# A transformer layer on one core: second-half feature blocks in three rounds, one copy on ScalarE, one low part on VectorE, two key scalings behind a weight split

## The chip, the cores and the metric

The kernel runs on one core of a Trainium2 chip. A core has five engines with a queue of instructions each: TensorE (PE: matrix products and transposes into PSUM), VectorE (DVE), ScalarE (ACT), GpSimd (POOL) and SyncE (SP, which here issues most of the transfers). The engines wait for one another by semaphores. The metric is the time of one execution on the device in microseconds, as a median over runs.

## The reference

One layer over 1024 latent tokens of width 1024 with 256 context tokens ahead of them. Cut to what matters here:

```python
h_lat = rms_norm(x, norm1_g) * (1 + sc1) + sh1        # sh1, sc1 from silu(c) @ w_mod + b_mod
h_ctx = rms_norm(ctx, norm1_g) * (1 + csc1) + csh1    # the same from c_ctx
rq, rk, rv, rg, dq, dk, dv = split(h @ w_in)          # seven blocks of 512 columns
# retention: rotary on rq, rk; per direction and head, over chunks of 128 tokens
S = S * c_dec + (kc * k_dec).T @ vc
o = (qc @ kc.T * intra) @ vc + (qc * q_dec) @ S
# differential attention: softmax(q1 k1) - lam * softmax(q2 k2), times dv
x = x + g1 * (concat(silu(rg) * norm(o), norm(att)) @ w_out)
x = x + g2 * conv_ffn(rms_norm(x, norm2_g) * (1 + sc2) + sh2)
out = rms_norm(x, final_g)
```

Everything is float32. The change lies in `h_lat` and `h_ctx` (the opening), and where the retention keys `rk`, the gates `rg` and the states `S` are computed.

## The kernel before, in words

**Products.** A float32 product is made of three passes (`passes`, lines 133 to 135): each operand is split into a high part of a shorter type (a copy or cast on ACT) and a low part, the difference (a subtraction on DVE), and PE adds high by high, high by low and low by high. So an operand is ready when its low part is.

**The opening.** The 1024 token rows are eight tiles of 128; tiles 0 to 3 are the first half (`xs0`), tiles 4 to 7 the second half (`xs1`). Each row tile gets its sum of squares on ACT (`square`, L561), a short DVE step and a power on POOL (`power`, lines 115 and 116: their result is the factor of the norm), and is scaled on DVE (`scale`, L567). Then `modulate` turns it over, one feature block d of 128 features at a time, for four tiles together: four transposes on PE into a PSUM buffer (`pt`, L573), the modulated high part on ACT (`hT`, L576), a modulated plain copy on DVE (`tmp`, L578), and the low part from copy and high part (L580) on DVE for d = 0, 1 and even d, on POOL for the other odd d. There are three transpose buffers `pt` and two copy buffers `tmp`, so a transpose can wait for the copy of three blocks earlier, and a copy for the low part of two blocks earlier. The second half's blocks are called B0 to B7 below, and the last one of the first half A7.

While the blocks are made, PE multiplies what is there: for k = 0 to 7 the products of feature block k for token tiles 0 and 1 and then for 2 and 3 (`part_products`, lines 617, 619 and 623, six products each time) with the block of w_in that holds the values of the differential attention. In the last two rounds, k = 6 and 7, the second half's blocks stand in pairs in front of these products: B0, B1 | B2, B3 | B4, B5 | B6, B7. Then come token tiles 4 and 5, three passes for each k (24 products each), with a function `between` that puts other work between them: in tile 4 the stores of token tiles 2 and 3 and the context's squares, powers and scalings, in tile 5 the context's eight feature blocks (`cT`, made by `modulate` too, two tiles together).

`in_order(begin)` holds PE, DVE, ACT and SP to the order in which the opening is written, up to the end of token tile 5. POOL is free of it. Outside of the opening a scheduler sets the order, and `order_only(a, b)` is a constraint for it: a comes after b, without a wait.

**Weights.** Each later block of w_in is streamed in four slices (`split_slice`): a load, the high part `whi` on ACT (L194), the low part `wlo` on DVE (L195).

**Retention keys and gates.** With the rotary tables in place, `transposed` makes the retention keys, for four heads in two token halves: 24 products into `pl`, then `rotated` (two ACT copies of half the partitions into `xb`, L443; the DVE steps `xa`, L449 and the following), and one tile later `natural_copy` turns the rotated tile over (`pk`, L461), copies it on ACT (L463) and stores it. Then the gates' block is streamed, and for its natural tiles (products `pn`) the function `states` runs beside: for each step of the recurrence it loads a tile `kvs` of keys and values that was stored before, scales the keys by their decay on ACT (`scaled_keys`, `ks`, L326), and multiplies (`pu`, L342).

Of the kernel before, what the change touches and what calls it, by code (L numbers as in the profile page):

```python
# [11 lines left out]
AF = mybir.ActivationFunctionType  # L12
ALU = mybir.AluOpType
# [4 lines left out]
P = 128  # L18
D = 1024
KD = D // P  # L20
# [54 lines left out]
def kernel(  # L75
# [81 lines left out]
    with ExitStack() as p1:  # L157
# [24 lines left out]
        mcol = hp.tile([P, KD, 2, 2], F32, name="mcol")  # L182
        csil = hp.tile([P, KD, 2], F32, name="csil")

        low_parts, newest_raw = [], []

        def split_slice(src, pool, spare=False):
            raw = ev.tile([P, 2, 512], F32, name="raw", tag="xhl") if spare else wr.tile([P, 2, 512], F32, name="raw")
            newest_raw[:] = newest_raw[-1:] + [nc.sync.dma_start(out=raw, in_=src)]
            if spare:  # L190
                order_only(newest_raw[1].ins, newest_raw[0].ins)
            whi = pool.tile([P, 2, 512], F32R, name="whi")
            wlo = pool.tile([P, 2, 512], F32R, name="wlo")
            nc.scalar.copy(whi, raw)  # L194
            low_parts.append(nc.vector.tensor_tensor(out=wlo, in0=raw, in1=r32(whi), op=ALU.subtract))  # L195
            return whi, wlo

# [49 lines left out]
        class Pair:  # L247
# [46 lines left out]
            def turn(self, behind=None):  # L294
# [9 lines left out]
                o = self.g % 2 * 2 * P  # L304
                nc.sync.dma_start(out=yr_d[self.g // 2][:, :, self.h, o : o + 2 * P].rearrange("p a (s l) -> p a s l", s=2), in_=r32(yr))

        states_at, last_y, turned_q, newest, first_turned, newest_read, rotations, made = {}, [], {}, [], [], [], [], {}

        def states(heads):


            one = [(0, 0, (0, 1)), (1, 0, (1, 0))]
            for g in range(1, 5):
                one += [(0, g, (0, 1) if g < 4 else (0,)), (1, 5 - g, (1, 0) if g < 4 else (1,))]
            seq = [(h, *step) for h in heads for step in one]
            kvs = []

            def load_until(n):
                for i in range(len(kvs), min(n, len(seq))):
                    h, d, g, _ = seq[i]  # L320
                    kvs.append(kvs[-1] if g == 0 and d == 1 else load_kv(h, g, "kvs", 0))

            def scaled_keys(i):
                h, d = seq[i][:2]
                ks = rt.tile([P, 2, P], F32, name="ks")
                nc.scalar.activation(ks, kvs[i][:, 0], AF.Copy, scale=kd[:, h, d : d + 1])  # L326
                return ks

            load_until(4)
            yield  # L330
            ahead = scaled_keys(0)
            for i, (h, d, g, cs) in enumerate(seq):
                if i % len(one) == 0:
                    states_at[h] = [rt.tile([P, NT, P], F32, name=f"S{e}") for e in range(2)]
                    last, made = [None, None], [-2, -2]
                load_until(i + 4)
                kv, ks = kvs[i], ahead
                if i + 1 < len(seq):
                    ahead = scaled_keys(i + 1)
                pu = tr_tile([P, 2, P], "pu")  # L340
                for c in cs:
                    mm(pu[:, c, :], ks[:, c, :], kv[:, 1, c, :], start=True, stop=True)  # L342
# [115 lines left out]
        def natural_copy(xa, h, hf):  # L458
            pk = pst.tile([P, 4, P], F32, name="pk", tag="tr")
            for i in range(4):  # L460
                nc.tensor.transpose(pk[:, i, :], xa[:, i * P : (i + 1) * P], ident)  # L461
            st = ev.tile([P, 4, P], F32, name="st")
            nc.scalar.copy(st, pk)  # L463
# [66 lines left out]
        with ExitStack() as p0:  # L530
# [35 lines left out]
            def scale(xt, col, c0=0, c1=D):  # L566
                nc.vector.tensor_scalar(out=xt[:, c0:c1], in0=xt[:, c0:c1], scalar1=sm[:, col : col + 1], scalar2=None, op0=ALU.mult)  # L567

            def modulate(tiles, d, who, hi, lo):
                n = len(tiles) * P  # L570
                pt = pst.tile([P, 512], F32, name="pt", tag="tr")
                for i, t in enumerate(tiles):
                    nc.tensor.transpose(pt[:, i * P : (i + 1) * P], t[:, d * P : (d + 1) * P], ident)  # L573
                sh = mcol[:, d, 0, who : who + 1]
                a = mcol[:, d, 1, who : who + 1]
                nc.scalar.activation(hi, pt[:, :n], AF.Identity, scale=a, bias=sh)  # L576
                tmp = xp.tile([P, 512], F32, name="tmp", bufs=2)
                nc.vector.tensor_scalar(out=tmp[:, :n], in0=pt[:, :n], scalar1=a, scalar2=sh, op0=ALU.mult, op1=ALU.add)  # L578
                eng = nc.gpsimd if d % 2 and d > 1 else nc.vector
                eng.tensor_tensor(out=lo, in0=tmp[:, :n], in1=r32(hi), op=ALU.subtract)  # L580

            mods, wts, rws = mm_tile("pr").rearrange("p (a b) -> p a b", a=2), {}, {}
# [96 lines left out]
            for k in range(KD):  # L679
# [21 lines left out]
                    scale(xs1[2], 8)  # L701
                    scale(xs1[3], 9)
                if k >= 6:
                    latents(1, 4 * (k - 6))
                    latents(1, 4 * (k - 6) + 1)
                if 0 < k < 5:
                    load_row(k + 3)
                n = k + 4
# [22 lines left out]
                    power(6)  # L731
                    power(7)
                if k == 4:
                    scale(xs1[1], 7)
                    square(xs1[3], 9)
                    power(9)
                if k == 5:
                    first.close()
                    cp = pctx.enter_context(tc.tile_pool(name="cp", bufs=1, side="right"))
# [2 lines left out]
                        xc.append(xp.tile([P, D], F32, name="xc", tag="wt", bufs=5))  # L742
                        nc.sync.dma_start(out=xc[t], in_=ctxt[t * P : (t + 1) * P, :])
                if k >= 6:
                    latents(1, 4 * (k - 6) + 2)
                    latents(1, 4 * (k - 6) + 3)
            rtab = load_rope(1)
            for t in range(2):
                store(t, part[t])

            def between(t, k):
                if (t, k) == (4, 1):
                    for i in (2, 3):
                        store(i, part[i])
                if t == 4 and k in (3, 5):
# [1009 lines left out]
```

## Time and profile before

| | us |
|---|---|
| median of three runs | 1378.36 (1378.05, 1378.36, 1380.14) |
| the profiled execution's own time | 1378.18 |
| its span, first to last instruction | 1376.4 |
| mean granted clock of PE | 0.998 |
| PE busy | 1358.7 (99%) |
| DVE, ACT, POOL busy | 1000.9, 730.7, 339.8 |

The page and the views of the trace tell times of one execution in microseconds from the span's start, and 1.8 us lie around the span. A row of busy times gives an engine, its time, its share of the span and its instructions. In a table by stage each row begins with the stretch A:B and its length; then follow, each with its instruction count, busy PE, PE's weight loads (PEld), DVE, ACT and POOL, then the granted clock, the busy share of the DMA engines and the GB/s. A wait is written "waiting instruction <- instruction that ended it: total, count, mean". In a table of rows in order of time each row has its start, its duration, engine, line, operation, output <- inputs with their shapes, and how many instructions follow one another there; a bracket at the end is the idle time ahead of it, and what ended it. For several instructions the duration runs from the first's start to the last's end. Groups give busy time and mean ns of one, then the engine's idle time ahead of them.

### The profile page before, as it was taken

The page shows a single profiled execution, that of the slowest core. Times are in us where ns is not written, and L with a number is a line of the kernel's source. Part 1 is how long each engine was busy: PE and PEld are TensorE (multiplying, and loading weights), DVE is VectorE, ACT ScalarE, POOL GpSimd, SP SyncE. Part 2 cuts the span into 40 slices and gives each one's busy share as a digit, 9 for nine tenths or more (in the row PEclk, how much of TensorE's full clock was granted, in tenths as well). Part 3 has the DMA queues.
Part 4 walks back from the last instruction along what each step waited for, and adds up shares of the span by engine and source line. Part 5 has one row for each costly group of instructions (what it writes and reads, how often), then busy time and mean ns, then how long its engine had stood idle before and what let it go on. Part 6 is the DMA issues. An engine that isn't in the chain of part 4 may idle for free.

```text
span 1376.4 us, 19496 instructions
## 1 busy us (share of the span) xinstructions
PE 1358.7 (99%) x7026; PEld 1143.8 (83%) x7026; DVE 1000.9 (73%) x1473; ACT 730.7 (53%) x1396; POOL 339.8 (25%) x375
## 2 busy tenths in 40 slices
PE   9999999999999999999999999999999999999997
PEld 6788888888988899998888778888888888888886
DVE  4655874425776998895458997878777887799857
ACT  4652312434665889985146554455544555454534
POOL 1310005403665424410201633322333220000001
PEclk9999999999999999999999999999999999999999
DMA  9546897654556767624410233233232325963523
GB/s 377 202 166 209 292 323 247 183 169 143 169 168 200 169 172 177 145 37 153 146 46 31 87 113 107 108 115 111 96 115 100 115 78 171 375 225 114 177 92 123
DMA packets 97192, 218.32 MB, mean 159 GB/s; under 512 B 9732, under 2 KB 31236, under 8 KB 96584
## 3 DMA queue, kind: packets, MB, share of 16 engines
q1 hardware_dynamic: 86216, 185.98, 39.6%
q0 software_dynamic: 10304, 29.65, 9.0%
q10 hardware_dynamic: 576, 1.44, 0.3%
q8 instruction: 55, 0.90, 0.3%
q14 instruction: 41, 0.34, 0.1%
HBM read 160.40 MB, written 56.64 MB: 158 GB/s over the span
## 4 chain that ended last, share of the span: by engine, by line
PE 90%; DVE 4%; DMA 2%; ACT 2%; issue 1%; SPq 0%; POOL 0%; POOLq 0%; ACTq 0%; DVEq 0%
PE chain L133 5%; PE chain L134 5%; PE chain L135 5%; PE pv L939 5%; PE pA L907 5%; PE c L134 5%; PE c L135 5%; PE c L133 5%; PE pl L135 4%; PE pl L133 4%; PE pl L134 4%; PE pn L135 3%; PE pn L134 3%; PE pn L133 3%; PE third L133 3%; PE third L135 3%
## 5 line engine op out<-in xcount | busy, mean ns | idle before, releaser
L133 PE MATMUL pl<-hT,whi 128*128 128x512 f32 x256 | 105.4, 412 | 0.0
L133 PE MATMUL chain<-T,whi 128*128 128x512 f32 x264 | 103.2, 391 | 2.2 <-ACT ua L1395 1.5
L134 PE MATMUL chain<-T,whi 128*128 128x512 f32 x264 | 102.9, 390 | 0.0
L135 PE MATMUL chain<-T,wlo 128*128 128x512 f32 x264 | 102.6, 389 | 0.0
L910 DVE TENSOR_REDUCE mt<-pA 128x1 f32<-128x1280 f32 x64 | 95.2, 1489 | 7.1 <-PE pA L907 6.8
L135 PE MATMUL pl<-hT,wlo 128*128 128x512 f32 x256 | 100.2, 391 | 0.0
L134 PE MATMUL pl<-hT,whi 128*128 128x512 f32 x256 | 100.0, 391 | 0.0
L135 PE MATMUL c<-whi,ghl 128*128 128x512 f32 x232 | 90.3, 389 | 0.0
L133 PE MATMUL c<-whi,ghl 128*128 128x512 f32 x232 | 90.3, 389 | 0.0
L134 PE MATMUL c<-wlo,ghl 128*128 128x512 f32 x232 | 90.3, 389 | 0.0
L907 PE MATMUL pA<-ks,qhl 128*128 128x512 f32 (+1 forms) x384 | 89.5, 368 | 0.6 <-ACT p L914 0.5
L914 ACT ACTIVATE p<-pA,mt 128x1280 f32<-128x1280 f32 x64 | 85.4, 1335 | 8.6 <-DVE mt L910 8.5
L1127 ACT CAST whi<-cmb 128x512 fp32r<-128x512 f32 x62 | 38.4, 622 | 82.0 <-PE chain L134 65.0
L1300 POOL TENSOR_TENSOR cmb<-wrb 128x512 f32<-128x512 f32 x19 | 26.6, 1400 | 223.6 <-DMA wrb<-w_up 134.5
L907 PEld LDWEIGHTS pA<-ks,qhl 128*128 128x128 f32 x384 | 67.9, 189 | 12.7 <-ACT p L914 1.3
L939 PE MATMUL pv<-va,aT 128*128 128x128 f32 x640 | 77.0, 276 | 0.2 <-ACT aT L933 0.2
L1130 DVE TENSOR_TENSOR wlo<-cmb,whi 128x512 fp32r<-128x512 f32 x62 | 60.2, 972 | 20.5 <-ACT whi L1127 20.5
L939 PEld LDWEIGHTS pv<-va,aT 128*128 128x128 f32 x640 | 74.0, 192 | 0.9 <-ACT aT L933 0.8
L1127 ACT CAST whi<-wra 128x512 fp32r<-128x512 f32 x54 | 33.1, 622 | 69.6 <-PE third L134 42.4
L133 PE MATMUL third<-yT,whi 128*128 128x512 f32 x168 | 65.6, 391 | 1.8 <-DVE ub L1404 1.8
L135 PE MATMUL third<-yT,wlo 128*128 128x512 f32 x168 | 65.5, 390 | 0.0
L134 PE MATMUL third<-yT,whi 128*128 128x512 f32 x168 | 65.5, 390 | 0.0
(331 smaller groups left out, 3878.2 us busy)
## 6 DMA issues: line engine op xcount, KB each, us to landing
wm<-w_mod SPq DMA_DIRECT2D x32, 512.0 KB, 5.2
raw<-w_in SPq DMA_DIRECT2D x27, 512.0 KB, 6.0
wra<-w_up SPq DMA_DIRECT2D x24, 512.0 KB, 3.3
wrb<-w_up SPq DMA_DIRECT2D x22, 512.0 KB, 3.5
W<-w_down SPq DMA_DIRECT2D x44, 256.0 KB, 6.5
ad<-s SPq DMA_DIRECT2D x20, 512.0 KB, 3.3
wra<-ad SPq DMA_DIRECT2D x20, 512.0 KB, 3.8
kvs<-kvg SPq DMA_DIRECT2D x36, 256.0 KB, 3.2
```

The costliest lines, as they stand in the source:

```text
L133: mm(ps, lh, rh, start=first, stop=False, skip_group_check=more)
L134: mm(ps, lh, rl, start=False, stop=False, skip_group_check=more)
L135: return mm(ps, ll, rh, start=False, stop=last, skip_group_check=more)
L907: mm(self.pa[m][:, c0:c1], self.q[:, m, i, qs], self.k[:, m, c0:c1], start=(i == 0), stop=(i == 1))
L910: nc.vector.tensor_reduce(out=self.mt[:, m : m + 1], in_=self.pa[m][:, :LK], axis=AX.X, op=ALU.min)
L914: nc.scalar.activation(self.p[m], self.pa[m][:, :LK], AF.Exp, scale=-1.0, bias=self.mt[:, m : m + 1], accum_out=self.s[:, m : m + 1])
L939: mm(self.pv, self.aT[:, c, :], self.v[:, c, :], start=(c == 0), stop=(c == NKT - 1))
L1127: cast = nc.scalar.copy(hi, src)
L1130: lows.append(nc.vector.tensor_tensor(out=lo, in0=src, in1=r32(hi), op=ALU.subtract))
L1300: nc.gpsimd.tensor_tensor(out=s1, in0=b1, in1=b2, op=ALU.add)
```

## The change

What it does:

1. Order of the scalings (k = 4): the square and the power of x tile 7 are written ahead of the scaling of tile 5, not behind it.
2. Rounds: the second half's blocks stand as B0 | B1, B2 | B3, B4 | B5 in the rounds k = 6 and 7, and B6 and B7 follow within token tile 4, after its second and its third k.
3. B4's plain copy is made on ACT, by the function that makes the high part, and not on DVE.
4. B7's low part is made on DVE, not on POOL.
5. The stores of token tiles 2 and 3 stand behind token tile 4's third k, not its second.
6. Three order constraints: the sixth key copy after the gates' first high part, the last but one rotation's first DVE step after the gates' first low part, and the first two key scalings after the second half copy of the last rotation. The first two name pairs that stood in this order before.

```diff
-            def modulate(tiles, d, who, hi, lo):
+            def modulate(tiles, d, who, hi, lo, late=False):
...
-                nc.vector.tensor_scalar(out=tmp[:, :n], in0=pt[:, :n], scalar1=a, scalar2=sh, op0=ALU.mult, op1=ALU.add)
-                eng = nc.gpsimd if d % 2 and d > 1 else nc.vector
+                if late and d == 4:
+                    nc.scalar.activation(tmp[:, :n], pt[:, :n], AF.Identity, scale=a, bias=sh)
+                else:
+                    nc.vector.tensor_scalar(out=tmp[:, :n], in0=pt[:, :n], scalar1=a, scalar2=sh, op0=ALU.mult, op1=ALU.add)
+                eng = nc.gpsimd if d % 2 and d > 1 and (d, late) != (KD - 1, True) else nc.vector
...
-                modulate((xs0, xs1)[half][t0:t1], d, 0, hT[0][half][:, d, t0 * P : t1 * P], hT[1][half][:, d, t0 * P : t1 * P])
+                modulate((xs0, xs1)[half][t0:t1], d, 0, hT[0][half][:, d, t0 * P : t1 * P], hT[1][half][:, d, t0 * P : t1 * P], half == 1)
...
                 if k >= 6:
-                    latents(1, 4 * (k - 6))
-                    latents(1, 4 * (k - 6) + 1)
+                    for d in ((0,), (3, 4))[k - 6]:
+                        latents(1, d)
...
                 if k == 4:
-                    scale(xs1[1], 7)
                     square(xs1[3], 9)
                     power(9)
+                    scale(xs1[1], 7)
...
                 if k >= 6:
-                    latents(1, 4 * (k - 6) + 2)
-                    latents(1, 4 * (k - 6) + 3)
+                    for d in ((1, 2), (5,))[k - 6]:
+                        latents(1, d)
...
             def between(t, k):
-                if (t, k) == (4, 1):
+                if t == 4 and 0 < k < 3:
+                    latents(1, k + 5)
+                if (t, k) == (4, 2):
                     for i in (2, 3):
                         store(i, part[i])
...
         last_rk = transposed(wg, rk_d, rtab, 64, RET_SCALE, 0, by_head, True)
+        slice0 = len(low_parts)
         wg = stream_block(3)
+        order_only(key_copies[5].ins, high_parts[slice0].ins)
+        order_only(rotations[-2][1].ins, low_parts[slice0].ins)
+        rk_turned = rotations[-1][0][1]
...
         order_only(copied_at[0], stops[first_stop].ins)
+        for made_key in keyed[:2]:
+            order_only(made_key.ins, rk_turned.ins)
```

What is left out of the diff collects the instructions that these constraints name (`high_parts`, `key_copies`, `keyed`).

PE in the opening, round k = 6, before: `pt_646` is B0 and `pt_655` B1; `pn_204` and `pn_205` are the products of token tiles 0 and 1, `hT00_177` the first half's high parts.

```order
L573 MATMUL pt_646<-ident_69,xs1_0_206 128x128
L573 MATMUL pt_646<-ident_69,xs1_1_207 128x128
L573 MATMUL pt_646<-ident_69,xs1_2_208 128x128
L573 MATMUL pt_646<-ident_69,xs1_3_209 128x128
L573 MATMUL pt_655<-ident_69,xs1_0_206 128x128
L573 MATMUL pt_655<-ident_69,xs1_1_207 128x128
L573 MATMUL pt_655<-ident_69,xs1_2_208 128x128
L573 MATMUL pt_655<-ident_69,xs1_3_209 128x128
L617 MATMUL pn_204<-whi_593,hT00_177 128x512
L617 MATMUL pn_205<-whi_593,hT00_177 128x512
```

The same place now, where `pt_661` is B1:

```order
L574 MATMUL pt_646<-ident_69,xs1_0_206 128x128
L574 MATMUL pt_646<-ident_69,xs1_1_207 128x128
L574 MATMUL pt_646<-ident_69,xs1_2_208 128x128
L574 MATMUL pt_646<-ident_69,xs1_3_209 128x128
L621 MATMUL pn_204<-whi_593,hT00_177 128x512
L621 MATMUL pn_205<-whi_593,hT00_177 128x512
L623 MATMUL pn_204<-wlo_594,hT00_177 128x512
L623 MATMUL pn_205<-wlo_594,hT00_177 128x512
L627 MATMUL pn_204<-whi_593,hT10_179 128x512
L627 MATMUL pn_205<-whi_593,hT10_179 128x512
L574 MATMUL pt_661<-ident_69,xs1_0_206 128x128
L574 MATMUL pt_661<-ident_69,xs1_1_207 128x128
```

B1 has moved behind the six products of token tiles 0 and 1, and so all later blocks by one place, the last two into token tile 4.

ACT from the second half's first high part to the first store of token tile 4, before: `hT_178` are the second half's high parts, `st` the copies of the stores, `sq,sm` the context's squares.

```order
L576 ACTIVATE hT_178<-pt,mcol 128x512 x8
L418 ACTIVATE st<-pn 128x512 x4
L561 ACTIVATE sq,sm<-xc 128x1024 x2
L418 ACTIVATE st<-pn 128x512
```

And now:

```order
L577 ACTIVATE hT_178<-pt,mcol 128x512 x5
L580 ACTIVATE tmp<-pt,mcol 128x512
L577 ACTIVATE hT_178<-pt,mcol 128x512
L419 ACTIVATE st<-pn 128x512 x2
L577 ACTIVATE hT_178<-pt,mcol 128x512 x2
L419 ACTIVATE st<-pn 128x512 x2
L562 ACTIVATE sq,sm<-xc 128x1024 x2
L419 ACTIVATE st<-pn 128x512
```

B4's copy is new behind its high part, and B6's and B7's high parts stand behind the first two stores.

ACT at the retention keys, before: `xb` are the half copies of the first rotations, `ks` the two key scalings, `st_2173` the copy of the first key tile.

```order
L443 ACTIVATE xb_2139<-pl_2113 64x512 x2
L326 ACTIVATE ks_2502<-kvs_2487,kd_882 128x256
L326 ACTIVATE ks_2506<-kvs_2487,kd_882 128x256
L463 COPY st_2173<-pk_2168 128x512
L443 ACTIVATE xb_2181<-pl_2146 64x512 x2
```

The rows with the scalings now, at the end of the keys, where `xb_2433` belongs to the last rotation, and `whi_2460` and `whi_2878` are high parts of streamed weights:

```order
L444 ACTIVATE xb_2433<-pl_2398 64x512 x2
L194 CAST whi_2460<-raw_2458 128x1024
L327 ACTIVATE ks_2502<-kvs_2487,kd_882 128x256
L327 ACTIVATE ks_2506<-kvs_2487,kd_882 128x256
L194 CAST whi_2878<-raw_2876 128x1024
L464 COPY st_2483<-pk_2478 128x512
```

The scalings have passed all copies and rotations of the keys and one weight split. Four short steps on the decay tables (128 by 128 and 128 by 1) on ACT have also passed two splits of the next block's weights, though no line of the diff names them.

More of the change, by code (lines that the diff above doesn't have):

```diff
@@ L183 @@
         csil = hp.tile([P, KD, 2], F32, name="csil")
-        low_parts, newest_raw = [], []
+        high_parts, low_parts, newest_raw = [], [], []
         def split_slice(src, pool, spare=False):
@@ L193, in split_slice @@
             wlo = pool.tile([P, 2, 512], F32R, name="wlo")
-            nc.scalar.copy(whi, raw)
+            high_parts.append(nc.scalar.copy(whi, raw))
             low_parts.append(nc.vector.tensor_tensor(out=wlo, in0=raw, in1=r32(whi), op=ALU.subtract))
@@ L305, in turn @@
                 nc.sync.dma_start(out=yr_d[self.g // 2][:, :, self.h, o : o + 2 * P].rearrange("p a (s l) -> p a s l", s=2), in_=r32(yr))
+        keyed, key_copies = [], []
         states_at, last_y, turned_q, newest, first_turned, newest_read, rotations, made = {}, [], {}, [], [], [], [], {}
@@ L325, in scaled_keys @@
                 ks = rt.tile([P, 2, P], F32, name="ks")
-                nc.scalar.activation(ks, kvs[i][:, 0], AF.Copy, scale=kd[:, h, d : d + 1])
+                keyed.append(nc.scalar.activation(ks, kvs[i][:, 0], AF.Copy, scale=kd[:, h, d : d + 1]))
                 return ks
@@ L462, in natural_copy @@
             st = ev.tile([P, 4, P], F32, name="st")
-            nc.scalar.copy(st, pk)
+            key_copies.append(nc.scalar.copy(st, pk))
             for i in range(2):
```

## The prediction

> **What bounds the kernel now.** I read the page's first part, then busy time by stage, then what TensorE (PE) waited for, and last the rows of time of the two places that the change touches.
>
> ```profile
> PE 1358.7 (99%) x7026; PEld 1143.8 (83%) x7026; DVE 1000.9 (73%) x1473; ACT 730.7 (53%) x1396; POOL 339.8 (25%) x375
> ...
> 45.98:64.20 18.22, 16.51 (x86) 12.55 (x86) 15.76 (x22) 10.66 (x17) 6.13 (x5) 1.00 0.57 212
> 219.00:268.00 49.00, 48.31 (x230) 39.45 (x229) 21.05 (x28) 18.71 (x30) 29.54 (x44) 1.00 0.58 178
> 64.20:219.00 154.80, 154.80 (x737) 130.06 (x736) 104.92 (x169) 51.73 (x98) 11.87 (x16) 1.00 0.73 251
> ```
>
> PE sets the time: 1358.7 of the 1376.4 us span. Of its 17.7 us of idle time the change can reach two pieces. One is the second half's feature blocks, 45.98 to 64.20 us, where PE lacks 18.22 - 16.51 = 1.71 us, the clock is granted in full, and VectorE (DVE) is nearly full, 15.76 of 18.22. The other is the retention keys and the first gate tiles, 219 to 268 us, 0.69 us. Between them PE never rests (154.80 of 154.80), so what the opening gains can arrive there whole.
>
> What PE waited for in the two:
>
> ```profile
> PE pt L573 <- DVE xs L567: 0.9, 1, 0.9
> PE pt L573 <- DVE tmp L578: 0.8, 1, 0.8
> PE pn L134 <- DVE wlo L195: 0.4, 1, 0.4
> PE pk L461 <- DVE xa L449: 0.3, 1, 0.3
> ```
>
> Two waits hold the opening, both for DVE: the scaling of x tile 7, and a scaled copy that still occupies a transpose buffer. I call the second half's feature blocks B0 to B7, and the first half's last one A7. PE's rows:
>
> ```profile
> 47.84 0.66 PE L573 MATMUL pt<-ident,xs 128*128 128x128 f32 x3
> 49.36 0.97 PE L573 MATMUL pt<-ident,xs 128*128 128x128 f32 x5 [0.86 <-DVE xs L567]
> ...
> 55.77 0.66 PE L573 MATMUL pt<-ident,xs 128*128 128x128 f32 x4 [0.79 <-DVE tmp L578]
> 56.19 0.70 PE L617 MATMUL pn<-whi,hT 128*128 128x512 f32 x2
> ...
> 57.65 1.04 PE L573 MATMUL pt<-ident,xs 128*128 128x128 f32 x8
> ...
> 63.87 0.50 PE L135 MATMUL pn<-whi,hT 128*128 128x512 f32 x1
> 64.20 0.40 PE L133 MATMUL pn<-whi,hT 128*128 128x512 f32 x1
> ```
>
> B0's first three transposes start at 47.84, the fourth at 49.36. B5 starts at 55.77, when B2's copy is done. The start at 64.20 belongs to the next token tile: it is the mark by which I measure the gain. A block's four transposes cost 0.42 us (55.77 to 56.19), six products 1.46 (56.19 to 57.65).
>
> **The change, part by part.**
>
> *Order of the scalings.* DVE and GpSimd (POOL) before B0:
>
> ```profile
> 46.08 0.20 ACT L561 ACTIVATION_READ_ACCUMULATOR sq<-xs 128x1 f32 x1
> 46.64 0.74 DVE L567 TENSOR_SCALAR xs<-xs,sm 128x1024 f32<-128x1024 f32 x1
> 47.30 0.14 DVE L115 TENSOR_SCALAR sm<-sm 128x1 f32<-128x1 f32 x1
> 47.53 0.99 POOL L116 TENSOR_TENSOR sm<-sm,mhalf 128x1 f32<-128x1 f32 x1 [4.29 <-DVE sm L115]
> 48.55 0.75 DVE L567 TENSOR_SCALAR xs<-xs,sm 128x1024 f32<-128x1024 f32 x1 [0.44 <-POOL sm L116]
> ```
>
> Tile 7's sum of squares is ready at 46.28 (46.08 + 0.20), but its small DVE step stands behind tile 5's scaling and runs at 47.30; the power follows on POOL until 48.52, and tile 7's scaling at 48.55. The change puts the small step first: 46.64 to 46.78, power to about 47.9, and DVE, doing tiles 5 and 6 meanwhile at 0.67 to 0.74 each, is free at about 48.1. Tile 7 is scaled by 48.85 instead of 49.30, and B0's fourth transpose starts at 48.9 instead of 49.36: **0.45 us**.
>
> *Rounds.* B0 stands alone now, then B1 and B2, B3 and B4, B5, and B6 and B7 within the first token tile's products. The same 32 transposes and the same products run; two more change-overs between them cost up to 0.1 us each. What counts is when DVE has freed each buffer (there are three):
>
> ```profile
> 50.84 1.53 DVE L578 TENSOR_SCALAR tmp<-pt,mcol 128x512 f32<-128x512 f32 x2
> 52.40 1.15 DVE L580 TENSOR_TENSOR hT<-tmp,hT 128x512 fp32r<-128x512 f32 x1
> 53.47 0.80 DVE L578 TENSOR_SCALAR tmp<-pt,mcol 128x512 f32<-128x512 f32 x1
> 54.92 0.80 DVE L578 TENSOR_SCALAR tmp<-pt,mcol 128x512 f32<-128x512 f32 x1
> ```
>
> That is DVE's chain of A7's and B0's copies, B0's low part, B1's copy and, after B1's low part, B2's copy, which freed B5 at 55.72. In the new order DVE starts it 0.45 to 0.55 earlier (A7's copy at 50.3, done 51.05), so B0's copy ends at 51.8, its low part at 52.95, B1's copy at 53.75, B2's at 55.2, B3's at 56.65. PE, by the prices above and 0.08 for each change-over: six products 49.0 to 50.5; B1 to 51.0; B2 must await A7's copy, 51.1 to 51.6; products to 53.05; B3 to 53.55; B4 must await B1's copy (53.75), 53.8 to 54.3; products to 55.75; B5, which awaits B2's copy of 55.2, without a wait to 56.25; two steps of the first token tile to 57.7; B6; one step; B7 done at 59.5; five more steps of three products (about 0.23 each) to 62.95. Against 64.20 that is **1.25 us**, tile 7's 0.45 included. PE's idle time there would fall from 1.71 to about 0.8: 0.4 before the fourth transpose, 0.1 and 0.25 before B2 and B4.
>
> *B4's copy on ScalarE (ACT), B7's low part on DVE.*
>
> ```profile
> L578 DVE TENSOR_SCALAR tmp<-pt,mcol 128x512 f32<-128x512 f32 x9 | 7.0, 802 | 0.1
> L576 ACT ACTIVATE hT<-pt,mcol 128x512 fp32r<-128x512 f32 x9 | 6.6, 777 | 5.9 <-PE pt L573 5.9
> L580 POOL TENSOR_TENSOR hT<-tmp,hT 128x512 fp32r<-128x512 f32 x4 | 5.1, 1286 | 10.2 <-DVE tmp L578 10.2
> L580 DVE TENSOR_TENSOR hT<-tmp,hT 128x512 fp32r<-128x512 f32 x5 | 4.8, 970 | 0.2
> ```
>
> ACT's form into the plain tile is not in this trace; its nearest row is the same function from the same buffer at 777 ns, DVE's own copy is 802. I take 0.78, with 0.62 to 1.0 as bounds. It leaves DVE 0.8 shorter and runs when B2's low part has freed the second copy buffer, 55.9 to 56.7, while PE reaches B6, which needs it, at 57.7. Queued behind it on ACT are B5's high part, the stores of token tiles 0 and 1, then B6's and B7's high parts; these end at about 60.3 and are needed at 62.2. B7's low part costs 0.69 to 1.15 on DVE in place of 1.29 on POOL and ends at about 62.4, needed at 62.7; before, it was the 0.1 us before 63.87. The skill's page "ScalarE: Activation LUTs", section "Rules for kernel authors", says that multiply and add belong on VectorE, which it calls up to about 3 times as fast in bf16. At three times 0.80 B4's copy would end near 58.3, B6 would wait 0.6, and the gain would be 0.65 (an estimate from that page); the 777 beside 802 ns speaks against it. The page "SBUF — State Buffer", section "Who interferes with whom", says that a DVE operation with two SBUF inputs and a GpSimd one that reads SBUF exclude each other for a whole instruction. The 1.15 us row began inside a POOL low part, so there is a clash, though less than a whole instruction's worth: 1286 ns is the longest that could be added and 0.46 was. By the rule each clash costs up to 0.14 more, B4 waits so much longer and the gain is 1.1.
>
> *Context behind it.* The squares of the two context tiles follow those stores on ACT, and PE transposes the context in the second token tile:
>
> ```profile
> 62.33 1.24 ACT L418 ACTIVATE st<-pn 128x512 f32<-128x512 f32 x2 [1.62 <-DMA dvd<-st]
> ...
> 67.13 0.76 DVE L567 TENSOR_SCALAR xc<-xc,sm 128x1024 f32<-128x1024 f32 x1 [0.45 <-POOL sm L116]
> ...
> 67.98 0.51 PE L573 MATMUL pt<-ident,xc 128*128 128x128 f32 x3
> ```
>
> This was just in time: scaled at 67.89, used at 67.98. Now PE comes at about 66.0 (1.25 for the gain, three products earlier in the new order). The first stores leave some 2 us earlier, so the third copy no longer waits for their DMA; I get the second context tile scaled at 65.9. This costs nothing or 0.2.
>
> *Weight slices of the next block.* The new order lets four short table steps of 0.3 us pass the last two slices on ACT:
>
> ```profile
> 93.76 1.04 ACT L194 CAST whi<-raw 128x1024 fp32r<-128x1024 f32 x1
> 93.59 2.47 DVE L195 TENSOR_TENSOR wlo<-raw,whi 128x1024 fp32r<-128x1024 f32 x2 [1.45 <-ACT whi L194]
> 97.87 0.39 PE L135 MATMUL pl<-hT,wlo 128*128 128x512 f32 x1
> ```
>
> The last low part is ready at 96.06 and needed at 97.87: 1.8 us of cover for about 0.9. All of it hangs on the context and shifts with PE. Nothing.
>
> *Key scalings and gates' slice.*
>
> ```profile
> 225.00 0.91 ACT L326 ACTIVATE ks<-kvs,kd 128x256 f32<-128x256 f32 x2 [4.48 <-DMA kvs<-kvg]
> ...
> 263.57 1.05 ACT L194 CAST whi<-raw 128x1024 fp32r<-128x1024 f32 x1 [1.12 <-DMA raw<-w_in]
> 265.93 0.50 PE L134 MATMUL pn<-wlo,hT 128*128 128x512 f32 x1 [0.43 <-DVE wlo L195]
> ...
> 267.64 1.06 PE L342 MATMUL pu<-kvs,ks 128*128 128x128 f32 x8
> ```
>
> Two scalings block ACT until 225.00 for their DMA; behind them the copies and rotations of the first key tiles are a microsecond late, for which PE has other products. Moved behind the split of 263.57 they run at 264.6 to 265.6, two us ahead of their use at 267.64. The 0.43 us wait hangs on the last slice's load, which the change does not touch; the first slice stands where it stood. I cost this at **0**; bounds are -0.7 (both waits gone) and +0.5 (the scalings, 0.91 us, in front of the last split's partner).
>
> **Sum.** 1.25 with 0.05 off for the context: 1.2 us. The profiled execution took 1378.18 (span 1376.4 and 1.8 around it), so 1377.0; the median of the runs shown is 0.18 above it, which gives **1377.2**.
>
> **Rivals.**
> - *Everything goes* (0.06): both waits of the opening with their refills (counted from start to start, 47.84 + 0.33 to 49.36 is 1.19, and 55.77 less 54.75 is 1.02; with the 0.1 and the change-overs about 2.4) and the second place's 0.7 vanish: 1378.36 - 3.1 = 1375.3. Against it: DVE must still do 15 us of work in that window.
> - *The stall only moves* (0.18): DVE is the limit; with clashes of 0.46 on three low parts its chain runs 0.8 late, B4, B6 and the context wait, and 0 to 0.6 remains: 1378.0.
> - *Slower* (0.10): ACT's queue. B4's copy waits there for DVE's B2 low part, and the stores stand ahead of B6 and B7. If DVE's chain is 1.3 us late or more, B5 to B7's high parts, stores, squares and context scaling are all late, and PE, at the context 1.9 us sooner, waits longer than it gained. If scaling stays at 67.89, the wait is 1.9 against 1.25: 1379.0. It decides from a context scaling after about 67.3.
> - *The change does nothing it says* (0.03): the order shows that it moves, so only the second place, where the slice's order is the same, is of this kind: 1378.4.
>
> **How the numbers follow.** The forecast (0.6 to 1.9 us gained, 1376.5 to 1377.8) has 0.63. The range 1375.3 to 1379.3 reaches from the first rival to the slower one, with 0.3 on top for the median's place (0.31 above the lowest of its runs). A difference of 0.2%, 2.8 us, is about what a measurement of this kernel tells from none, and nearly all of the cases lie inside: faster by more needs everything to go, 0.05; slower by more 0.04; within it 0.91.
>
> **What would show it.** Right: in PE's rows the fourth transpose of B0 about 0.45 earlier, waits there of 0.3 to 0.5, short waits before B2 and B4, the next token tile at 62.8 to 63.3, no wait of more than 0.2 at the context, and the 0.4 for the gates' last slice still there. Wrong: a wait for ACT's copy before B6, a context wait above 0.5, or a PE wait between 64 and 219 us, where none was.

## The result, and the profile after

| | runs | median, us | lowest to highest | mean |
|---|---|---|---|---|
| before | 22 | 1380.10 | 1377.94 to 1383.35 | 1380.34 |
| changed | 22 | 1377.35 | 1376.44 to 1379.67 | 1377.57 |

The ratio is 0.9980, with a 95% interval of 0.9973 to 0.9987: 1.8 to 3.7 us faster. The profiled execution of the changed kernel took 1376.93 us (span 1375.2), 1.25 less than the one of before. So the two profiled executions differ by what was forecast, and the medians by more than twice as much; the runs of before are also spread wider, over 5.4 us against 3.2. The three runs that the prediction started from (median 1378.36) were a low sample of these 22. When the two kernels ran again, on one chip, their medians lay 1.85 us apart (ratio 0.9987, further down). One execution of 1947.74 us, of the kernel before with a later load, had a granted clock of 0.655 and is left out below.

The page's first part and the table by stage of the changed kernel, in the columns of before:

```profile
PE 1357.8 (99%) x7026; PEld 1143.1 (83%) x7026; DVE 1001.9 (73%) x1473; ACT 731.3 (53%) x1397; POOL 345.7 (25%) x374
...
45.98:64.20 18.22, 17.18 (x90) 13.25 (x90) 17.01 (x25) 13.35 (x22) 6.11 (x6) 1.00 0.64 232
64.20:219.00 154.80, 154.80 (x737) 130.00 (x736) 104.19 (x167) 50.49 (x95) 10.76 (x14) 1.00 0.73 247
219.00:268.00 49.00, 48.71 (x233) 39.90 (x232) 24.18 (x31) 19.46 (x31) 32.25 (x44) 1.00 0.64 188
```

PE lacks 18.22 - 17.18 = 1.04 us in the first stretch, where it lacked 1.71, still nothing in the second, and 0.29 in the third, where it lacked 0.69. PE's rows of the opening:

```profile
47.76 0.65 PE L574 MATMUL pt<-ident,xs 128*128 128x128 f32 x3
48.91 0.33 PE L574 MATMUL pt<-ident,xs 128*128 128x128 f32 x1 [0.50 <-DVE xs L568]
...
51.26 0.65 PE L574 MATMUL pt<-ident,xs 128*128 128x128 f32 x4 [0.19 <-DVE tmp L582]
...
62.81 0.50 PE L135 MATMUL pn<-whi,hT 128*128 128x512 f32 x1 [0.25 <-DVE sm L115]
63.16 0.40 PE L133 MATMUL pn<-whi,hT 128*128 128x512 f32 x1
```

B0's fourth transpose starts at 48.91 (forecast 48.9), B2 at 51.26 (51.1), the next token tile at 63.16 (62.95). PE's weight loads (PEld) show two waits more plainly:

```profile
53.90 0.42 PEld L574 LDWEIGHTS pt<-ident,xs 128*128 128x128 f32 x4 [0.34 <-DVE tmp L582]
...
62.81 0.19 PEld L135 LDWEIGHTS pn<-whi,hT 128*128 128x128 f32 x1 [0.67 <-DVE hT L584]
```

The first is B4, which waits for B1's copy, done at 53.84. PE's own rows hide it, because B3's and B4's eight transposes stand there as one row; they take 1.11 us (53.20 to 54.31), where eight took 0.79 before (57.65 to 58.44). The second is the last product, which waits for B7's low part: 0.25 us in PE's row, 0.1 before. PE's row names the short step that VectorE began as that part ended. The opening starts up to 0.9 us earlier or later from one execution to another, so from here on the opening is measured as **the stretch**, from B0's first transpose to the next token tile: 47.84 to 64.20 or 16.36 us before, 47.76 to 63.16 or 15.40 changed. It repeats well: 16.36 or 16.37 in the three traces with the opening of before, 15.39 or 15.40 in the four with the changed one.

### The profile page after: what moved, and what is told of

The parts are those of the page before. It is cut to its first block, busy times and chain, and to the rows that moved or that the text cites. A ratio compares the mean times of both kernels' runs of the same rounds, so it can differ in the third digit from the quotient of the medians.

```text
span 1375.2 us, 19497 instructions
## 1 busy us (share of the span) xinstructions
PE 1357.8 (99%) x7026; PEld 1143.1 (83%) x7026; DVE 1001.9 (73%) x1473; ACT 731.3 (53%) x1397; POOL 345.7 (25%) x374
## 4 chain that ended last, share of the span: by engine, by line
PE 90%; DVE 4%; DMA 2%; issue 2%; ACT 2%; SPq 0%; POOL 0%; POOLq 0%; DVEq 0%; ACTq 0%
PE pv L951 5%; PE chain L133 5%; PE chain L134 5%; PE chain L135 5%; PE pA L919 5%; PE c L134 5%; PE c L133 5%; PE c L135 5%; PE pl L133 4%; PE pl L135 4%; PE pl L134 4%; PE pn L135 3%; PE pn L134 3%; PE pn L133 3%; PE third L133 3%; PE third L135 3%
```

## The experiments

**The two halves of the change, and a later load.** Theory A: beyond the opening, the runs gained what ACT's wait for the keys' load cost PE in most executions, though hardly in the profiled one. Theory B: all of it comes from the opening. Four kernels on one chip, beside 33 runs of before (median 1378.94, mean 1379.41, 1377.53 to 1383.99).

The order constraints alone, on the kernel before:

```diff
+        order_only(key_copies[5].ins, high_parts[slice0].ins)
+        order_only(rotations[-2][1].ins, low_parts[slice0].ins)
...
+        for made_key in keyed[:2]:
+            order_only(made_key.ins, rk_turned.ins)
```

> The kernel before with the three order constraints alone: every engine's order is that of before, except that ACT's first two key scalings stand behind the last rotation and one weight split. Theory A (what the runs gained beyond the opening is a wait for a transfer: ACT stood at these scalings until their keys had landed, in the profiled execution with 0.6 us to spare for PE, in others longer): the median falls by 1.0 to 2.0 us, the lowest run by no more than 0.4, and the runs spread less (highest at most 3.5 us over the lowest, against 5.4 before). Theory B (all of the gain comes from the opening): within 0.4 us of before, with before's spread. In the trace both expect the 0.26 us wait before the first key tile's transposes to stay within 0.3 us of what it was.

Median 1377.88, mean 1378.02, 1376.96 to 1379.17; ratio 0.9991 (0.9982 to 1.0000). The median fell by 1.06, the mean by 1.39, the spread from 6.5 to 2.2 us. The interval reaches 1, so the median alone would not settle it. The lowest run fell by 0.57, a little more than A allowed. The wait of 0.36 before the first key tile stayed in its trace.

The changed kernel with these same lines taken out:

> The changed kernel without the three order constraints: the opening is the changed one, the two key scalings stand where they stood before. Theory A: 1.0 to 1.4 us faster than before in median and in the lowest run, with the spread of before. Theory B: 2.4 to 3.0 us faster in median. In the trace both expect the next token tile to start at 63.0 to 63.3 us.

Median 1379.04, mean 1379.02, 1376.62 to 1382.39; ratio 0.9994 (0.9983 to 1.0005). The stretch is 15.40 (47.59 to 62.99), and yet the median did not fall at all, the mean by 0.39; only the lowest run fell, by 0.91. Both theories had the median too fast. The spread stayed, as A says. Its profiled execution happened to be the longest of its runs, 1382.39 us, and shows where the time goes. What PE waited for, longest first, with total, times and longest wait (the third number is the longest, not the mean):

```profile
PE pk L462 <- DVE xa L450: 2.2, 1, 2.2
...
PE pyt L297 <- POOL y L292: 1.1, 2, 0.6
```

Its rows on SP and ACT, and PE's second key tile:

```profile
214.50 0.52 SPq L425 DMA_DIRECT2D kvg<-st  x1
218.11 1.20 ACT L444 ACTIVATE xb<-pl 64x512 f32<-64x512 f32 x2 [4.11 <-PE pl L135]
222.80 0.33 SPq L238 DMA_DIRECT2D kvs<-kvg  x1
225.86 0.91 ACT L327 ACTIVATE ks<-kvs,kd 128x256 f32<-128x256 f32 x2 [6.55 <-DMA kvs<-kvg]
226.67 0.57 ACT L464 COPY st<-pk 128x512 f32<-128x512 f32 x1
227.26 1.20 ACT L444 ACTIVATE xb<-pl 64x512 f32<-64x512 f32 x2
...
230.97 1.11 PE L462 MATMUL pk<-ident,xa 128*128 128x128 f32 x4 [2.23 <-DVE xa L450]
```

The load `kvs` reads back what the store `kvg` of 214.50 wrote and waits for it: 8.3 us here. The same rows of the kernel before:

```profile
215.77 0.52 SPq L424 DMA_DIRECT2D kvg<-st  x1
219.32 1.20 ACT L443 ACTIVATE xb<-pl 64x512 f32<-64x512 f32 x2 [4.01 <-PE pl L135]
222.20 0.33 SPq L238 DMA_DIRECT2D kvs<-kvg  x1
...
226.40 1.19 ACT L443 ACTIVATE xb<-pl 64x512 f32<-64x512 f32 x2
...
228.95 0.69 DVE L449 TENSOR_TENSOR xa<-xa,xb 128x512 f32<-128x512 f32 x1
...
230.26 0.60 PE L461 MATMUL pk<-ident,xa 128*128 128x128 f32 x4
```

There the store took 6.4 us, and the scalings stood at 225.00. In the 14 traces of this case the store landed 6.4 to 9.5 us after its issue, and the 6.4 of the trace that the prediction read is the shortest. The load came 2.9 us after ACT's first rotation there; in the other eleven traces in which it was not delayed on purpose it came 3.0 to 7.1 us after it in ten, and 2.5 in one. PE reached the first rotation 1.2 us earlier in the opening's kernel (218.11 for 219.32), but the keys landed 0.86 later (225.86 for 225.00): the landing does not follow PE. So ACT starts the second rotation at 227.26, and PE waits 2.23. What the opening gains is handed over to this wait in such an execution.

The wait cost more than itself. Busy PE with its instructions, then the granted clock, the DMA engines' share and GB/s, around its end:

```profile
229.00:231.00 2.00, 0.03 (x1) 0.93 0.62 170
231.00:233.00 2.00, 2.00 (x7) 0.50 0.64 234
233.00:235.00 2.00, 2.00 (x8) 0.72 0.39 133
```

The clock was granted at half behind the wait. The four transposes and the six products after them took 3.34 us (230.97 to 234.31); behind a wait of 1.49, in the next kernel, the same ten took 1.88 (231.78 to 233.66) at a clock of 1.00. The wait and this 1.46 make 3.7 of the 5.5 us by which this execution is longer than the profiled one of the changed kernel. Whether other long executions lose clock in this way is not shown.

The wait on POOL's `y` in the list is another: it stands in 2 of the 14 traces of this case, and was not tried. The other one is the changed kernel with the old order of the scalings (below), with 1.4 us of it in an execution of 1380.26 us. There the key scalings are out of the way, so not all of the spread is theirs.

The kernel before with the load later:

```diff
+            if nm == "kvs" and not kv_loads:
+                order_only(load.ins, rk_stores[0].ins)
...
+        order_only(key_copies[0].ins, keyed[1].ins)
+        order_only(second_half[0].ins, keyed[1].ins)
```

> The kernel before, with the first load for the key scalings issued behind the first rotated keys' store (224.3 us) in place of ahead of it (222.2); ACT's order is that of before. The load lands about 2.3 us later. Theory A: ACT stands that much longer, the second rotation's halves come at 228.7 in place of 226.4, and PE, which had 0.6 us to spare at the second key tile's transposes (230.26), waits about 1.7 there: the median is 1.3 to 2.3 us above before. Theory B: PE has other products and the median stays within 0.5 us of before.

Median 1379.32, mean 1379.79, 1378.55 to 1382.16; ratio 1.0003 (0.9994 to 1.0012). Its trace has the wait where it was expected, and nearly as long (the last two lines are the landing time of the store of 215.09, and the stretch behind the wait in the columns of the table above):

```profile
224.09 0.33 SPq L240 DMA_DIRECT2D kvs<-kvg  x1
227.07 0.91 ACT L332 ACTIVATE ks<-kvs,kd 128x256 f32<-128x256 f32 x2 [6.67 <-DMA kvs<-kvg]
228.47 1.20 ACT L449 ACTIVATE xb<-pl 64x512 f32<-64x512 f32 x2
...
231.78 0.65 PE L467 MATMUL pk<-ident,xa 128*128 128x128 f32 x4 [1.49 <-DVE xa L455]
...
DMA to landing us min/median/max: 8.3/8.3/8.3
...
231.00:233.00 2.00, 1.22 (x8) 1.00 0.71 224
```

The median rose by 0.4 only, a miss for A's 1.3 to 2.3 and within the 0.5 of B, although B's reason does not hold in the trace, where PE waits 1.49. In this execution the store, issued at 215.09, took 8.3 us to land. So the load could not have gone before 223.4 in any case, and the delay to 224.09 cost it 0.7 us and not the 2.3 expected. A reading that fits: in many runs of before the load is late already, so a delay to a fixed point adds little to them. It is shown for this one execution only.

The same delay in the changed kernel:

> The changed kernel with the same load delayed in the same way; the scalings stand behind the last rotation, near 264 us, 35 us after the load. Both theories: within 0.5 us of the changed kernel, so 2.3 to 3.2 us below before. If it loses more than that, the delay itself costs elsewhere (SP's queue), and the run before says nothing on ACT's wait.

Median 1377.04, mean 1377.33; ratio 0.9987 (0.9978 to 0.9996): 1.9 us below before, less than the 2.3 to 3.2 expected, and the same ratio as the changed kernel's own when it ran again (below). With the scalings out of the way the late load costs nothing that can be seen. **A fits better than B**, on the spread of the first run, the wait in the second and third, the landings of 14 traces, and this one. It is not proven: the first run's interval reaches 1, and the third run's median missed. By means, against the same 33 runs: constraints alone -1.4, opening alone -0.4, both (with the later load) -2.1. That the two help each other is likely from the traces; the intervals don't prove it.

**The opening's parts.** All are edits of the changed kernel, on one chip, beside 35 runs of before (median 1379.56).

```diff
                 if k == 4:
+                    scale(xs1[1], 7)
                     square(xs1[3], 9)
                     power(9)
-                    scale(xs1[1], 7)
```

> The changed kernel with the scalings in the old order (the scaling of x tile 5 ahead of tile 7's small step); all else changed. The measure is PE's time from B0's first transpose to the next token tile, 16.36 us before and 15.40 in the changed kernel (47.76 to 63.16). Theory (the swap gives its 0.45): 15.7 to 15.9, with a wait of 0.8 to 0.95 for the last scaling; the median 0.3 to 0.5 above the changed kernel. Rival (VectorE's chain is the limit and takes the swap's gain back at B2 and B7): at most 15.5.

The wait for the last scaling is 0.87 in place of 0.50, the stretch 15.75 (48.44 to 64.19): the swap gives 0.35 to 0.37. Median 1378.21, ratio 0.9985 (0.9973 to 0.9997).

```diff
-                eng = nc.gpsimd if d % 2 and d > 1 and (d, late) != (KD - 1, True) else nc.vector
+                eng = nc.gpsimd if d % 2 and d > 1 else nc.vector
```

> The changed kernel with B7's low part on POOL, as before. Theory (POOL's 1.29 us for VectorE's 0.69, behind a copy that is done at 62.03, needed by PE at 62.40): PE waits 0.85 to 1.1 for it in place of 0.25, and the stretch from B0's first transpose to the next token tile is 16.0 to 16.3 in place of 15.40. Rival (PE waited for VectorE's queue, which gets 0.6 shorter, and not for the low part as such): at most 15.5.

```profile
63.69 0.50 PE L135 MATMUL pn<-whi,hT 128*128 128x512 f32 x1 [0.90 <-POOL hT L584]
64.03 0.40 PE L133 MATMUL pn<-whi,hT 128*128 128x512 f32 x1
```

The wait is 0.90, the stretch 16.02 (48.01 to 64.03): moving B7's low part gives 0.62. Yet the median is 1377.37 (ratio 0.9980, 0.9970 to 0.9991), no higher than the changed kernel's 1377.35 in other runs: the opening's loss can't be seen at the end.

```diff
-                if late and d == 4:
+                if late and d == KD:
```

> The changed kernel with B4's plain copy on VectorE, as before (the scheduler then also moves two products of a later tile and one weight split past short steps behind the opening). Theory (VectorE is without a pause from B0 on, so each copy that it makes moves its end by 0.8): B7's low part ends 0.7 to 0.9 later and the stretch is 16.0 to 16.3 in place of 15.40, the median 0.6 to 0.9 above the changed kernel. Rival (the copy was hidden either way): at most 15.6.

The stretch is 15.39 (48.07 to 63.46), the same as with ACT's copy, and the rival holds: B4's copy on ACT gives the opening **nothing**. Median 1377.86, ratio 0.9982 (0.9971 to 0.9994). VectorE's and POOL's rows in the changed kernel say why: B3's copy, B3's low part on POOL, B4's low part, and two more copies.

```profile
55.93 0.80 DVE L582 TENSOR_SCALAR tmp<-pt,mcol 128x512 f32<-128x512 f32 x1
56.82 1.29 POOL L584 TENSOR_TENSOR hT<-tmp,hT 128x512 fp32r<-128x512 f32 x1 [4.24 <-DVE tmp L582]
56.86 1.80 DVE L584 TENSOR_TENSOR hT<-tmp,hT 128x512 fp32r<-128x512 f32 x1
58.58 1.52 DVE L582 TENSOR_SCALAR tmp<-pt,mcol 128x512 f32<-128x512 f32 x2
```

And with B4's copy on VectorE:

```profile
56.25 1.52 DVE L582 TENSOR_SCALAR tmp<-pt,mcol 128x512 f32<-128x512 f32 x2
57.13 1.29 POOL L584 TENSOR_TENSOR hT<-tmp,hT 128x512 fp32r<-128x512 f32 x1 [4.25 <-DVE tmp L582]
57.81 1.17 DVE L584 TENSOR_TENSOR hT<-tmp,hT 128x512 fp32r<-128x512 f32 x1
```

B4's low part ends at 58.66 in the one (56.86 + 1.80) and 58.98 in the other, both 0.55 to 0.56 after POOL's end (58.11, 58.42); the second execution runs 0.31 later. A copy from PSUM runs beside POOL at full speed (1.52 for two); a low part, with two SBUF inputs, does not. So VectorE, freed of the copy, began B4's low part earlier and stood through POOL's part instead.

```diff
-                    scale(xs1[3], 9)
+                    scale(xs1[3], 9, 0, P)
+                    scale(xs1[3], 9, P, D)
...
-                if late and d == 4:
+                if late and d in (4, 6):
```

> The changed kernel with two further edits: the last scaling (x tile 7) is made in two pieces, B0's 128 columns first, and B6's plain copy is made on ACT too, as B4's is. Theory (what is left of the waits is VectorE's): the wait of 0.50 for the last scaling falls to 0.1 or less, that of 0.25 for B7's low part to 0, and the stretch from B0's first transpose to the next token tile is 14.6 to 15.0 in place of 15.40; the median 0.4 to 0.8 below the changed kernel. Rival (ACT's queue, longer by 0.8, delays B7's high part, the stores and the context): 15.4 or more, or a new wait at the context's transposes.

The wait for the last scaling went from 0.50 to below 0.1, that before B2 grew from 0.19 to 0.79, and the stretch is 15.51: a miss. The stretch lies where the rival had it, but not for the rival's reason, since the wait moved to B2 and the one for B7's low part stayed at 0.24. What fed B2 was not the scaling. Median 1378.49, mean 1378.32, ratio 0.9985 (0.9973 to 0.9997).

The medians of these four kernels do not follow their stretches: 16.02 goes with 1377.37, 15.39 with 1377.86, 15.75 with 1378.21 and 15.51 with 1378.49. The changed kernel itself did not run beside them. What each part is worth in the opening is shown, what it is worth at the end is not.

**What is left in the opening.** Two edits and the changed kernel again, beside 27 runs of before (median 1378.73).

```diff
-                eng = nc.gpsimd if d % 2 and d > 1 and (d, late) != (KD - 1, True) else nc.vector
+                eng = nc.gpsimd if d % 2 and d > 1 and not (late and d in (3, KD - 1)) else nc.vector
```

> The changed kernel with B3's low part on VectorE in place of POOL. In the traces so far a VectorE low part takes 0.69 us alone, but ends 0.54 to 0.55 after a POOL low part that it meets (the one of B4: 1.80 us). Theory (the two exclude each other, so POOL's 1.29 us stand in VectorE's way and moving B3's part costs 0.69 and saves 1.11): B4's low part takes 0.69, B7's ends about 0.4 earlier, the 0.25 us wait for it is gone and the stretch from B0's first transpose to the next token tile is 15.1 to 15.2 in place of 15.40. Rival (POOL's part ran for free and VectorE gets 0.69 more): the wait grows to 0.8 to 1.0 and the stretch to 16.0 or more.

```profile
55.86 0.81 DVE L582 TENSOR_SCALAR tmp<-pt,mcol 128x512 f32<-128x512 f32 x1
56.70 1.29 DVE L584 TENSOR_TENSOR hT<-tmp,hT 128x512 fp32r<-128x512 f32 x2
57.91 0.81 DVE L582 TENSOR_SCALAR tmp<-pt,mcol 128x512 f32<-128x512 f32 x1
```

Two low parts together take 1.29 us on VectorE, less than the one took beside POOL. The wait for B7 is gone and the stretch is 14.87 (47.67 to 62.54), better than the 15.1 to 15.2 expected. **Median 1376.21**, 1375.89 to 1377.28; ratio 0.9979 (0.9969 to 0.9988). That is 0.67 below the changed kernel beside it, and the fastest kernel of this case.

```diff
-                    scale(xs1[3], 9)
+                    scale(xs1[3], 9, 0, P)
+                    scale(xs1[3], 9, P, D)
...
         wg = stream_block(5)
+        order_only(low_parts[0].ins, last_scaled[0].ins)
```

> The changed kernel with two edits: VectorE's low part of the next block's first weight slice (1.22 us at 49.08, ahead of A7's copy, needed after 85 us) stands behind the second context tile's scaling, and the last scaling is made in two pieces, B0's 128 columns first. Theory (the waits that are left in the opening are all VectorE's chain, which starts with that slice): the waits of 0.50, 0.19 and 0.25 fall to 0.1 or less each, and the stretch from B0's first transpose to the next token tile is 14.4 to 14.8 in place of 15.40. If what the opening gains arrives at the end, the median is 0.5 to 1.0 below the changed kernel run beside it; if the next places that hang on transfers or on POOL (the gates' last slice near 264 us, the first retention pair near 322) take it back, within 0.3. Rival: the slice's later load makes block 5 wait near 85 to 100 us.

Stretch 15.53, median 1377.11 (ratio 0.9985, 0.9976 to 0.9994): the theory failed. VectorE's rows before A7's copy, and ACT's:

```profile
49.11 0.21 DVE L558 TENSOR_SCALAR mcol<-pm,cl 128x2 f32<-128x2 f32 x1
50.54 0.81 DVE L582 TENSOR_SCALAR tmp<-pt,mcol 128x512 f32<-128x512 f32 x1 [1.22 <-ACT hT L577]
```

```profile
49.73 1.45 ACT L577 ACTIVATE hT<-pt,mcol 128x512 fp32r<-128x512 f32 x2 [2.57 <-DVE mcol L558]
```

Where the slice stood, VectorE now idles for just as long. A7's copy waits for A7's high part, which waits for A7's two factors `mcol`, which VectorE makes behind all the scalings.

> The changed kernel itself, beside the two others: a median of 1376.9 to 1377.7, its highest run at most 3.5 above its lowest, and 1.5 to 3.0 us below the kernel before.

Median 1376.88, 1376.27 to 1377.95; ratio 0.9987 (0.9978 to 0.9996). Stretch 15.39.

The last kernel joins these: B3's low part on VectorE, the slice behind the context, and

```diff
-                    scale(xs1[3], 9)
...
                     mod_sums(k + 2)
+                    if k == 5:
+                        scale(xs1[3], 9, 0, P)
+                        scale(xs1[3], 9, P, D)
                     latents(0, k + 2)
```

> The changed kernel with B3's low part on VectorE, the next block's slice behind the context, and the last scaling, in two pieces (B0's 128 columns first), behind the two short steps that make block A7's factors. The run with the slice behind the context showed VectorE idle for 1.22 us in the slice's place: A7's copy waited for A7's high part on ACT, and that for the factors, which VectorE makes behind all scalings (49.1 us). Theory (these factors start the chain of copies): A7's high part starts at 48.5 in place of 49.6, its copy at 49.3 in place of 50.4, the 0.19 us wait before B2 is gone and the one for the last scaling 0.4 or less; the stretch from B0's first transpose to the next token tile is 14.4 to 14.7 in place of 15.40 in the changed kernel and 14.87 with B3's part alone, and the median 0.2 to 0.5 below that one's, against the kernel before 0.9970 to 0.9980. Rival (the copies hang on something else again): 14.85 or more and no gain over B3's part alone.

```profile
47.90 0.65 PE L574 MATMUL pt<-ident,xs 128*128 128x128 f32 x3
48.73 0.33 PE L574 MATMUL pt<-ident,xs 128*128 128x128 f32 x1 [0.18 <-DVE xs L568]
...
65.00 0.55 PE L574 MATMUL pt<-ident,xc 128*128 128x128 f32 x3 [0.30 <-DVE xc L568]
```

The stretch is 14.01 (47.90 to 61.91), below what was expected, and only the wait of 0.18 is left in PE's rows (B4's weight loads still wait 0.28): the factors did start the chain. But the median is 1376.99, 1375.54 to 1378.05 (ratio 0.9985, 0.9976 to 0.9994, beside 15 runs of before with median 1378.75): 0.8 above B3's part alone, with an opening 0.9 us shorter. The two ran on different chips and the intervals of their ratios overlap, so it is not shown that this kernel is slower; the further 0.2 to 0.5 us that was expected did not show either. In its profiled execution (1376.04) the context's transposes now wait 0.30, the gates' last slice 0.23 and the first retention pair 0.26, of which the kernel with B3's part alone shows none. That accounts for much of one execution, not for the wider spread, and why the shorter opening brings nothing at the end stays open.

## Why the prediction was right or wrong

The time (1377.2 forecast, 1377.35 measured) lies in the range, and the ratio at the edge of the 0.2% that the likeliest case stayed within. But the gain was forecast **too small**: 1.2 us, against 2.75 between medians (interval 1.8 to 3.7) and 1.85 when both kernels ran again (0.6 to 3.0). That the time came out to 0.15 us is luck: the start was 1.74 too low against the 22 runs, and the gain 1.55 too small.

- *Key scalings at 0*: **this is the step that failed**. I wrote that behind them copies and rotations come a microsecond late, "for which PE has other products". In the profiled execution it had, with 0.6 us to spare (the second tile's sum is ready at 228.95 + 0.69 = 229.64, PE comes at 230.26). But the store ahead of this load took 6.4 us there and up to 9.5 in the other 13 traces, so I had read the shortest of them. The constraints alone gave 1.1 (median) to 1.4 us (mean); with the opening's 0.96 that makes 2.1 to 2.4, between the two measured gains. My bound of -0.7 counted only the waits of one execution.
- *Order of the scalings, 0.45*: nearly right, 0.35 to 0.37.
- *Rounds, 1.25 with the scalings*: 1.04 by the start of the next token tile, 0.96 by the stretch. B2's wait came (0.19 for 0.1) and so did B4's (0.34 in the weight loads, 0.25 forecast), and B7's low part, for which I had 62.4 against 62.7, ended at 62.76 against 62.40.
- *B4's copy on ACT*: I let it shorten VectorE's chain by 0.8. It shortened nothing, since B4's low part then met POOL's: 1.80 us. I also had B6 need that copy's buffer; with three buffers it is B7.
- *Clash of VectorE and POOL*: I judged it "less than a whole instruction's worth" from one row that began halfway into a POOL part. The row that began with one was lengthened by 1.80 - 0.69 = 1.11 us, and moving that POOL part away freed it. The Trainium skill's page "SBUF — State Buffer", section "Who interferes with whom", excludes a VectorE operation with two SBUF inputs from running beside a GpSimd one that reads SBUF, and leaves one with at most one such input alone, outside the modes in which it uses both of its port pairs; the trace agrees in both (a low part ends 0.55 us after POOL's; two copies take 1.52 beside it). The gain of 1.1 worked out by that rule was nearer than my 1.25, though that working added 0.14 for each clash and foresaw none of 1.11.
- *ACT's price, 0.78*: right, as its row shows:

```profile
56.05 0.78 ACT L580 ACTIVATE tmp<-pt,mcol 128x512 f32<-128x512 f32 x1 [0.68 <-DVE hT L584]
```

- *B7's low part on VectorE, context, weight slices*: 0.69 us; no wait at the context; no wait of PE from 64.20 to 219 us. Right. That what the opening gains "can arrive there whole" is not shown: the stretches and the medians of the four parts go their own ways. The wait for the gates' last slice stayed, 0.20 for 0.43.
- *Rivals*: "the stall only moves" holds for pieces (the copy on ACT, the split scaling). ACT's queue, the slower rival, was never late.

## What to carry to other kernels

An instruction that waits for a transfer on an engine's in-order queue is priced by the spread of its landing over executions, not by the idle time beside it in one trace: look for what stands behind it, how much cover that has, and whether the landing follows the engine that is being made faster. Before an operation is moved to a freer engine, look whether the engine it leaves will then only wait longer for an instruction of another engine. And when removing the work ahead of a late step leaves idle time of the same length, the work was filling a wait: follow that step's own inputs.

## What the runs showed that I had not expected

- A store and the load that reads it back: 6.4 us from the store's issue to the load's issue in one execution and 8.3 in another, and about 3 us more to the landing (222.20 to 225.00, 222.80 to 225.86), while PE came 1.2 us earlier. Over 14 traces the store alone took 6.4 to 9.5.
- A wait of 2.23 us on PE was followed by a granted clock of 0.50 and 1.46 us of slower work, a wait of 1.49 by a clock of 1.00.
- One VectorE low part beside POOL takes 1.80 us, two without POOL 1.29.
- The opening of 14.01 us ends no earlier, by its median, than the one of 14.87.
